# Output projection of the last layer: program order for 696 of its 768 products, squares, sums and turns at fixed products, splits moved out of the query blocks

## The chip, the cores and the metric

One core of one Trainium2 chip runs the whole step. The metric is the device time in microseconds (us) from start to end of one execution. The engines of the core are TensorE (PE in the profile, its weight loads PEld), VectorE (DVE), ScalarE (ACT), GpSimd (POOL) and SyncE (SP), which here issues the DMA transfers.

## The reference

A trunk of two layers is run once on a prompt (512 rows) and a sample (32 rows), 544 columns in all where the kernel works on the transposed rows. Layer 0 is RWKV-7 time mixing, layer 1 differential attention with 12 heads of width 128; both have cross-attention over 256 memory rows with 4 heads, and a gate. What the change touches is the end of layer 1 and the final norm:

```
def diff_layer(x, ...):
    h = rmsnorm(x, norm_w)
    q, k, v, qm, gate = split(h @ w_in)            # widths 1536, 1536, 1536, 512, 2048
    o = rmsnorm(diff_attention(q, k, v, lam), subln) * (1.0 - lam_init)
    y_mem = mem_attention(qm, mk, mv)
    out = concatenate([o, y_mem]) * silu(gate)     # 2048 columns
    return x + out @ w_out, k, v                   # w_out: 2048 x 1024

y_prompt = rmsnorm(xp, final_norm_w)
y_sample = rmsnorm(xs, final_norm_w)
```

## The kernel before

**Products.** Every product with weights is split into float16 halves: a weight block of 1024 rows and 128 columns becomes a high part (cast) and a low part (what the cast lost), and the activations likewise. A product with 128 weight rows is then three matmuls: high by high, high by low, low by high. The 544 columns are taken in two halves of 272, so a block is 2 x 8 x 3 = 48 matmuls; the text counts these matmuls as products. The accumulator of a half is one of three PSUM banks (`psg`).

**Weight stream.** `stream` runs all blocks of layer 1 one after the other: per head a value, a key and a query block, gate blocks (`GATES1`; head 11 has four) and, in heads 1, 3, 5 and 7, memory blocks; then the 16 blocks of the output projection. While PE works on block b, other engines prepare later ones, each step tied to a product of block b: two loads of 256 KB into one of four raw buffers (`LOADS1`, SP), the squares of a raw block for its scale (`square_total`, at products 14 and 27, ACT, written to `junkw`), a small matmul that sums them (`total_spread`, PE), four scalar operations that make a power of two of it (`scales`, at 32, DVE), the scaling of the raw block in two pieces (`scaled`, POOL), and in the block after that the split: two casts (ACT, at 7 and 11 in the output projection, `SPLITS2`), two low parts (POOL and DVE, at 13 and 17), written to `whs`. A raw buffer is free for the next load when its split is done.

**Heads.** `diff_layer` lists the work beside the stream as events, `at(position, function)`; a position is a product, counted from the start of the layer, and `begin(h)` is that of head h. Scores of a head in four tiles, maxima (`snm`, DVE), exponentials (ACT), the turned weights and the sums of values follow at fixed offsets, in the head after their own as a rule.

**Gated tiles.** `o1` holds 16 tiles of 128 rows and 544 columns, the concatenated output by its gate. Each is split too: `gated_square` (ACT) and `gated_scales` find a scale, `gated_split` casts the scaled tile (ACT, first half of `hl`), `gated_rest` takes the low half (DVE, second half of `hl`). For tiles 0 to 7 these are events of heads 8 to 11, the splits by the offsets `GSPLIT` from head 10; tiles 8 to 15 are split in the output projection.

**Output projection.** `make_out` (in `diff_layer`) does 8 column blocks k with tiles 0 to 7 (q = 0) and then 8 with tiles 8 to 15 (q = 1), 768 products. After each half `out_add` adds the accumulator to the residual `x1` (DVE), and with q = 1 calls `consume` (in `layer1`) for the final norm: `square_sums` squares the new `x1` (ACT, into `sqn`) and adds it to `sums` (DVE); after k = 3 all five row tiles are turned for their first 512 columns (four transposes each, PE, into `ps_f`, of which `psm` has two buffers) and multiplied by the norm's weight `fw` (DVE); later blocks are turned near the end, where `last` makes the root (`token_rms`) and writes the output. The block k = 6 of q = 1 has only its first half at its own place; its second half lies between the two halves of k = 7.

**Order.** While `ordered` is set, each engine keeps the order in which the program issues its instructions (`tie`). Where it isn't, the language's planner orders an engine's instructions by its own estimate of when each can start; `tied` keeps SP's order in all cases. `layer1` drives the projection's products with a counter `n` (768 at the end; the events of the heads still take its first 93). A list `left` holds functions by product: squares, scales and splits of tiles 8 to 15, and six pairs of copies of keys and values to the output (`kv_out`, SP). After product 384, the end of q = 0, `ordered` is cleared:

```
if n == KT * 6 * KT:
    self.ordered, self.tied = False, (self.se,)
```

Of the kernel before, what the change touches and what calls it, by code (L numbers as in the profile page):

```python
# [3 lines left out]

# [5 lines left out]
F32 = mybir.dt.float32  # L10
# [4 lines left out]
AF = mybir.ActivationFunctionType  # L15
ALU = mybir.AluOpType
AX = mybir.AxisListType

P = 128
D = 1024  # L20
KT = D // P
# [3 lines left out]
TH = T // 2  # L25
# [20 lines left out]
GSQUARE = ((8, 36), (8, 132), (9, 36), (9, 84), (10, 2), (10, 29), (10, 53), (10, 75))  # L46
GSCALE = ((9, 132), (10, 92))
KVOUT = 164
GSPLIT, GREST = (37, 66, 84, 115, 134, 180, 227, 252), 11
EXP = float(1 << 23)  # L50
ROOT = float(0x5F3759DF) + 14 * EXP
SAMPLE1 = ((310, "s"), (338, "m"), (362, "t"), (386, "w"), (406, "n"), (464, "r"))
# [87 lines left out]
class Trunk:  # L140
# [1711 lines left out]
    def layer1(self):  # L1852
        nc, a, o = self.nc, self.a, self.o
        w = a["df_in"][0]
        op = self.pool("o1", 1)
        self.o1 = [op.tile([P, T], F32, name=f"og{g}") for g in range(16)]
        with ExitStack() as ectx:
            tiles, late = {}, []
            with ExitStack() as c2:
                dq = self.pool("dq", 1)  # L1860
                p = self.pool("df", 1, ctx=c2)
                mctx = ExitStack()
                mp = self.pool("mem1a", 1, ctx=mctx, side="right")

                self.kz = [dq.tile([P, 2, T], F32R, name=f"kz{i}") for i in range(2)]
                for t in self.kz:
                    for m in range(2):
                        r = slice(64 - 64 * m, P - 64 * m)
                        nc.gpsimd.memset(t[r, m, :].bitcast(F32), 0.0)
                self.out = {x: dq.tile([P, n], F32, name=f"out{x}") for x, n in (("s", 16), ("m", 2), ("c", 2))}  # L1870
                self.out["t"] = dq.tile([P, 16], BF16, name="outt")
                self.out["r"] = dq.tile([P, 2, KT], F32, name="outr")
                self.out["f"] = dq.tile([P, 4, KT], F32, name="outf")
                main, n, kv_out = self.diff_layer(dq, p, mp, mctx, lambda: self.pool("wo1e", 1, ctx=ectx, side="right"), tiles,
                                                  lambda *x: self.out_add(late, *x))
            ctx = ectx.enter_context(ExitStack())
            po = self.pool("wo1", 1, ctx=ctx)
            p = self.pool("fin", 1, ctx=ctx, side="right")
            self.all_ones(p)
            fw = p.tile([P, D], F32, name="fw")  # L1880
            nc.scalar.dma_start(fw[:], a["final_norm_w"].unsqueeze(0).to_broadcast([P, D]))
            sums = p.tile([P, T], F32, name="sums")
            ya, yb = ([t[:, :512] for t in self.o1[i : i + 5]] for i in (0, 5))
            rows = [P] * 4 + [TS]

            held = {}

            def bank(i, q, g):
                held[i] = q.tile([P, 512], F32, tag=g, name="ps_f")

            def turned(i, ks):
                for k in ks:
                    c = min(i * P, T - P)
                    self.te.transpose(held[i][:, k % 4 * P : k % 4 * P + P], self.x1[:, k, c : c + P], self.ident[:])
                return slice(P - rows[i], P), held.pop(i) if ks[-1] % 4 == 3 else None

            def last(tiles):

                rs = self.token_rms(sums, p, tiles)
                for u, i in enumerate(tiles):  # L1900
                    if i == 3:
                        bank(3, self.psm, "m")
                    n, pf = turned(i, range(4, KT) if i == 3 else (KT - 1,))
                    r = rs[n, u : u + 1]
                    dst = o[0][0, i * P : i * P + P, :] if i < 4 else o[1][0]
                    self.ae.activation(ya[i][n], ya[i][n], AF.Copy, scale=r)
                    self.se.dma_start(dst[:, :512], ya[i][n])
                    self.ve.scalar_tensor_tensor(yb[i][n], pf[n, :], r, fw[n, 512:], ALU.mult, ALU.mult)
                    self.se.dma_start(dst[:, 512:], yb[i][n])

            def consume(k, x, v):
                self.square_sums((k, x, v), p, sums)
                if k == 3 and v.start:
                    for i in range(5):
                        bank(i, self.psm, "m")
                        n, pf = turned(i, range(4))
                        self.ve.tensor_tensor(ya[i][n], pf[n, :], fw[n, :512], ALU.mult)
                if k == KT - 2:
                    for i, q, g in (((2, self.psc, "c"), (4, self.psc, "c")) if v.start else ((0, self.psm, "m"), (1, self.psm, "m"))):
                        bank(i, q, g)  # L1920
                        turned(i, (4, 5, 6))
                if k == KT - 1:
                    last((2, 3, 4) if v.start else (0, 1))

            late.append(consume)
            order = (12, 13, 14, 15, 8, 9, 10, 11)
            left = [(24 + 12 * i, self.gated_square, g) for i, g in enumerate(order)]
            left += [(126, lambda g: self.gated_scales(g, 8), 8), (138, self.half_scale, 1)]
            left += [(150 + 24 * i, lambda g: self.gated_split(g, po, tiles), g) for i, g in enumerate(order)]
            left += [(160 + 24 * i, lambda g: self.gated_rest(g, tiles), g) for i, g in enumerate(order)]  # L1930
            left += [(KVOUT + 48 * i, lambda i: kv_out[i](), i) for i in range(len(kv_out))]
            left.sort(key=lambda x: x[0])
            for _ in main:
                n += 1
                while left and left[0][0] <= n:
                    _, fn, g = left.pop(0)
                    fn(g)
                if n == KT * 6 * KT:
                    self.ordered, self.tied = False, (self.se,)
        self.hctx.close()  # L1940

# [64 lines left out]
    def diff_layer(self, dq, p, mp, mctx, pool_early, tiles, consume):  # L2006
# [6 lines left out]
        rows = [slice(0, 64), slice(64, P)]  # L2013

        def at(pos, fn):
            ev.append((pos, len(ev), fn))

        def begin(h):
            return 6 * KT * sum(3 + len(GATES1.get(x, ())) + 2 * (x in MEM1) for x in range(h))
# [89 lines left out]
        def bank(m, name):  # L2109
            pool, tag = ((self.psx, "x"), (self.psc, "c"))[m]  # L2110
            return pool.tile([P, 512], F32, tag=tag, name=name)
# [25 lines left out]
        def joined(st, t):  # L2137
            mixed(*st["pt", t])
            if t == 3:
                s0 = st["G"]["s0"][:, 4 * st["j"] : 4 * st["j"] + 4]  # L2140
                self.ve.reciprocal(s0, s0)

        def turned(st, t):
            b0 = 2 * t * (t + 1)
            joined(st, t)
            self.ve.transpose(st["pk"][:, b0 : b0 + 4 * (t + 1)].rearrange("p b c -> p (b c)"), st.pop(("pt", t))[0])
# [37 lines left out]
        def squared(st):  # L2184
            j = st["j"]
            self.ve.tensor_reduce(st["G"]["ss"][:, 0, 4 * j : 4 * j + 4], st.pop("sq")[:], AX.X, ALU.add)
# [127 lines left out]
        for h, st in enumerate(sts):  # L2314
            f, hg, G = len(makes) * 6 * KT, h // 4, groups[h // 4]
# [18 lines left out]
            back, sums = (BACK2, SUMS2) if h >= DH - 2 else (BACK1, SUMS1)  # L2334
# [4 lines left out]
            if h in MEM1:  # L2339
                m = MEM1.index(h)  # L2340
# [3 lines left out]
            if h % 4 == 3:  # L2344
                for off, fn in (SAMPLE2 if last else SAMPLE1):
                    fn = {"s": sample_scores, "m": sample_mixed, "t": sample_turned, "w": sample_weighted, "n": sample_norm, "r": sample_rows}[fn]
# [3 lines left out]
                for j in range(4):  # L2350
# [6 lines left out]
                    else:  # L2357
                        x = b + 18 + STEP * j
# [4 lines left out]
            if h == 10:  # L2363
                we = []
                at(f + 34, lambda: (mctx.close(), we.append(pool_early())))
                for g, off in enumerate(GSPLIT):
                    at(f + off, lambda g=g: self.gated_split(g, we[0], tiles))
                    at(f + off + GREST, lambda g=g: self.gated_rest(g, tiles))
        for g, (h, off) in enumerate(GSQUARE):
            at(begin(h) + off, lambda g=g: self.gated_square(g))  # L2370
        for g, (h, off) in zip((0, 4), GSCALE):
            at(begin(h) + off, lambda g=g: self.gated_scales(g, 4))
        at(begin(11) + 40, lambda: self.half_scale(0))
# [2 lines left out]
        first = len(makes) * 6 * KT  # L2376
# [30 lines left out]
        i = 0  # L2407
# [94 lines left out]
```

## Time and profile before

| What | us |
|---|---|
| Median of 3 runs (lowest to highest) | 1365.05 (1363.4 to 1370.18) |
| Profiled execution, its whole time | 1367.86 |
| its span, from the first to the last instruction | 1366.0 |
| PE busy | 1300.2 |
| DVE busy | 945.2 |
| ACT busy | 887.7 |
| POOL busy | 679.6 |

The profile is that of one execution, so its times are compared with its own span, and results with the runs. "Idle before, releaser" behind an instruction tells how long its engine had stood and which instruction's end let it go on. In the weight stream ps_g is the accumulator, ps_s the scores, whs a split weight block, h16s the raw blocks and their scales, hl a split gated tile, og a tile of `o1` (its room serves the output later), qp the query.

### The profile page before, as it was taken

Reading aid. Unit: us, or ns where it says so; the run is one execution under the profiler, and the core shown is the slowest. Engines: PE = TensorE matmul, PEld = TensorE weight load, DVE = VectorE, ACT = ScalarE, POOL = GpSimd, SP = SyncE. Lnnn points to the kernel's source line nnn. Section 1 sums busy time; section 2 is a strip of 40 time slices with the busy share of each in tenths; the row PEclk is TensorE's granted clock in tenths of the full one; section 3 lists DMA queues with packets and bytes.
Section 4 is the critical chain, followed back from the end, with each engine's and each line's share of the span. In section 5 each row is a group of like instructions: output and inputs, shape, how many; then the busy total and the mean of one; then the engine's idle time right before and its main releaser. Section 6 shows DMA issues by size and latency. Waiting matters only on the chain. (4 is left out here: it accounts for less than half of the span.)

```text
span 1366.0 us, 32365 instructions
## 1 busy us (share of the span) xinstructions
PE 1300.2 (95%) x11776; PEld 1170.6 (86%) x11776; DVE 945.2 (69%) x2477; ACT 887.7 (65%) x2412; POOL 679.6 (50%) x1145
## 2 busy tenths in 40 slices
PE   6998999999999999999999999999999999999987
PEld 6898889999999999888899997788878887778865
DVE  7766667877788778756683463666697667877745
ACT  7665777677777777665653356767766777775642
POOL 2216765568556755660120028665565655553641
PEclk9999999999999999999999999999999999999998
DMA  7542223322332232233366445767777868683731
GB/s 242 174 125 69 60 70 87 79 75 68 86 78 72 73 87 74 67 96 88 109 208 190 129 143 138 167 150 171 163 172 155 187 144 196 152 174 84 257 96 66
DMA packets 418298, 171.55 MB, mean 126 GB/s; under 512 B 195209, under 2 KB 402578, under 8 KB 418138
## 3 DMA queue, kind: packets, MB, share of 16 engines
q1 hardware_dynamic: 417994, 168.96, 47.9%
q8 instruction: 93, 1.52, 0.5%
q14 instruction: 67, 0.55, 0.1%
q10 hardware_dynamic: 144, 0.52, 0.1%
HBM read 130.84 MB, written 41.92 MB: 126 GB/s over the span
## 5 line engine op out<-in xcount | busy, mean ns | idle before, releaser
L137 PEld LDWEIGHTS <-whs 128*128 128x128 f16 x3456 | 330.2, 99 | 76.8 <-POOL whs L137 8.0
L137 PE MATMUL ps_g<-h,whs 128*128 128x272 f16 x2688 | 337.2, 282 | 3.5 <-POOL whs L137 3.5
L137 PE MATMUL ps_g<-hh,wlo 128*128 128x272 f32 x912 | 277.1, 304 | 1.2 <-DVE wlo L137 1.2
L137 PE MATMUL ps_g<-hh,whi 128*128 128x272 f32 x912 | 274.3, 301 | 0.9 <-ACT hh L137 0.9
L137 PE MATMUL ps_g<-hl,whi 128*128 128x272 f32 x912 | 270.9, 297 | 0.6 <-POOL hl L600 0.5
L889 POOL TENSOR_TENSOR tm<-u,m 102x84 f32<-102x84 f32 (+23 forms) x372 | 159.3, 428 | 165.3 <-DMA m<-sc 134.4
L137 POOL TENSOR_TENSOR whs<-h16s,whs 128x512 f16<-128x512 f32 x128 | 149.1, 1182 | 63.8 <-ACT whs L137 62.2
L137 PEld LDWEIGHTS ps_g<-hh,whi 128*128 128x128 f32 x912 | 174.1, 191 | 4.4 <-ACT hh L137 1.3
L137 PEld LDWEIGHTS ps_g<-hh,wlo 128*128 128x128 f32 x912 | 173.6, 190 | 4.7 <-DVE wlo L137 2.0
L137 PEld LDWEIGHTS ps_g<-hl,whi 128*128 128x128 f32 x912 | 173.5, 190 | 2.4 <-POOL hl L600 0.7
L891 POOL TENSOR_TENSOR u<-u,tm 102x84 f32<-102x84 f32 (+23 forms) x372 | 159.5, 429 | 29.1
L137 DVE TENSOR_TENSOR wlo<-raw,whi 128x512 fp32r<-128x512 f32 x178 | 129.3, 737 | 47.4 <-ACT whi L137 46.5
L137 ACT CAST whi<-raw 128x512 fp32r<-128x512 f32 x178 | 107.1, 616 | 35.8 <-issue 19.3
L137 POOL TENSOR_SCALAR h16s<-h16s 128x512 f32<-128x512 f32 x112 | 78.8, 715 | 96.7 <-DVE h16s L137 89.1
L137 ACT CAST whs<-h16s 128x512 f16<-128x512 f32 x144 | 84.2, 617 | 31.0 <-POOL h16s L137 25.5
L137 PE MATMUL ps_g<-hl,whs 128*128 128x272 f16 x768 | 93.8, 279 | 3.3 <-POOL whs L137 2.2
L137 ACT ACTIVATE junkw<-h16s 128x512 bf16<-128x512 f32 x138 | 86.6, 627 | 9.4 <-DMA h16s<-in_w_out_dram 9.0
L137 DVE SCALAR_TENSOR_TENSOR SB<-ps_c,dl,sd 64x64 f32<-64x64 f32 x168 | 47.4, 282 | 43.0 <-PE ps_c L137 38.6
L137 PE MATMUL ps_g<-lo,whi 128*128 128x272 f32 x256 | 73.9, 289 | 0.7 <-DVE lo L137 0.7
L137 PE MATMUL ps_g<-hi,whi 128*128 128x272 f32 x256 | 73.7, 288 | 0.0
L137 PE MATMUL ps_g<-hi,wlo 128*128 128x272 f32 x256 | 73.6, 288 | 0.0
L137 ACT COPY sv<-ps_c 64x64 f32<-64x64 f32 x192 | 39.2, 204 | 39.2 <-PE ps_c L137 37.4
(413 smaller groups left out, 2926.6 us busy)
## 6 DMA issues: line engine op xcount, KB each, us to landing
raw<-in_rw_in_dram SPq DMA_DIRECT2D x114, 256.0 KB
h16s<-in_df_in_dram SPq DMA_DIRECT2D x112, 256.0 KB
raw<-in_w_out_dram SPq DMA_DIRECT2D x32, 256.0 KB
h16s<-in_w_out_dram SPq DMA_DIRECT2D x32, 256.0 KB
ptr<-pk SPq DMA_DIRECT2D x44, 160.0 KB
aT<-ptr SPq DMA_DIRECT2D x11, 640.0 KB
scr<-sg SPq DMA_DIRECT2D x96, 68.0 KB
out_dram<-scr SPq DMA_DIRECT2D x6, 1024.0 KB
```

Of the source, the lines that this page charges most:

```text
L137: return lambda *a, **k: self.trunk.tie(self, issue(*a, **k))
L889: nc.gpsimd.tensor_tensor(tm[:, :n, :wd], u3[:, :n, kx : kx + 1].to_broadcast(sh), m3[:, kx : kx + 1, kx + 1 :].to_broadcast(sh), ALU.mult)
L891: nc.gpsimd.tensor_tensor(u3[:, :n, kx + 1 :], u3[:, :n, kx + 1 :], tm[:, :n, :wd], ALU.add)
```

## The change

Three edits go together.

- The splits of tiles 0 to 7 get places by head and product, one for the cast and one for the low half, instead of offsets from head 10 with a fixed distance of 11. The casts move from products 37, 66, 84, 115, 134, 180, 227 and 252 of head 10 (which has 144, head 11 follows) to 36 and 66 of head 10 and 33, 66, 165, 222, 254 and 290 of head 11; the low halves follow by 7 to 24 products.
- `ordered` is cleared at product 696 (`ORDERED`) instead of 384. From there 72 products are left: the two halves of k = 7 and the second of k = 6.
- In `consume` the square is issued one product later and its sum eight products later, through the list `left`, which can now take new entries while it runs; the first turns of row tile i are issued at 6 + 14 i products behind k = 3, and the product with `fw` 7 behind them, where before all five stood together. The squares and sums of the last three halves stay at once.

```diff
-from itertools import chain
+from itertools import chain, count
-GSPLIT, GREST = (37, 66, 84, 115, 134, 180, 227, 252), 11
+GSPLIT = ((10, 36, 57), (10, 66, 89), (11, 33, 57), (11, 66, 89), (11, 165, 172), (11, 222, 230), (11, 254, 262), (11, 290, 298))
+ORDERED = (2 * KT - 2) * 6 * KT + 3 * KT
...
-            held = {}
+            held, left, ticket = {}, [], count()
+
+            def after(off, fn, g):
+                left.append((n + off, next(ticket), fn, g))
+
+            def squared(x):
+                k, t, v = x
+                sq = sums[:, v]
+                if k:
+                    held["sq"] = p.tile([P, TH], F32, tag="sqn", name="sqn", bufs=2)
+                    sq = held["sq"][:]
+                self.ae.activation(sq, t, AF.Square)
+
+            def summed(v):
+                self.ve.tensor_tensor(sums[:, v], sums[:, v], held["sq"][:], ALU.add)
+
+            def first(i):
+                bank(i, self.psm, "m")
+                held["p", i] = turned(i, range(4))
+
+            def weighed(i):
+                rows, pf = held["p", i]
+                self.ve.tensor_tensor(ya[i][rows], pf[rows, :], fw[rows, :512], ALU.mult)
...
             def consume(k, x, v):
-                self.square_sums((k, x, v), p, sums)
                 if k == 3 and v.start:
                     for i in range(5):
-                        bank(i, self.psm, "m")
-                        n, pf = turned(i, range(4))
-                        self.ve.tensor_tensor(ya[i][n], pf[n, :], fw[n, :512], ALU.mult)
+                        after(6 + 14 * i, first, i)
+                        after(13 + 14 * i, weighed, i)
+                if k < KT - 2 or k == KT - 2 and not v.start:
+                    after(1, squared, (k, x, v))
+                    if k:
+                        after(8, summed, v)
+                else:
+                    squared((k, x, v))
+                    summed(v)
...
-            left.sort(key=lambda x: x[0])
             for _ in main:
                 n += 1
+                left.sort()
                 while left and left[0][0] <= n:
-                    _, fn, g = left.pop(0)
+                    _, _, fn, g = left.pop(0)
                     fn(g)
-                if n == KT * 6 * KT:
+                if n == ORDERED:
                     self.ordered, self.tied = False, (self.se,)
...
-                for g, off in enumerate(GSPLIT):
-                    at(f + off, lambda g=g: self.gated_split(g, we[0], tiles))
-                    at(f + off + GREST, lambda g=g: self.gated_rest(g, tiles))
...
+        for g, (h, x, y) in enumerate(GSPLIT):
+            at(begin(h) + x, lambda g=g: self.gated_split(g, we[0], tiles))
+            at(begin(h) + y, lambda g=g: self.gated_rest(g, tiles))
```

The left-out lines fill `left` with the same functions at the same products as before.

More of the change, by code (lines that the diff above doesn't have):

```diff
@@ L1925, in layer1 @@
             late.append(consume)
[L1926 to L1931, printed above, removed]
-            left.sort(key=lambda x: x[0])
+            n0, n = n, 0
+            for i, g in enumerate((12, 13, 14, 15, 8, 9, 10, 11)):
+                after(24 + 12 * i, self.gated_square, g)
+                after(150 + 24 * i, lambda g: self.gated_split(g, po, tiles), g)
+                after(160 + 24 * i, lambda g: self.gated_rest(g, tiles), g)
+            after(126, lambda g: self.gated_scales(g, 8), 8)
+            after(138, self.half_scale, 1)
+            for i in range(len(kv_out)):
+                after(KVOUT + 48 * i, lambda i: kv_out[i](), i)
+            n = n0
             for _ in main:
                 n += 1
+                left.sort()
                 while left and left[0][0] <= n:
-                    _, fn, g = left.pop(0)
+                    _, _, fn, g = left.pop(0)
                     fn(g)
-                if n == KT * 6 * KT:
+                if n == ORDERED:
                     self.ordered, self.tied = False, (self.se,)
```

## The prediction

> **What bounds the kernel now.** I read the page first, then the busy time by stretch of the span, then who TensorE (PE) waited for, then the timeline of the two places where it did.
>
> ```profile
> span 1366.0 us, 32365 instructions
> PE 1300.2 (95%) x11776; PEld 1170.6 (86%) x11776; DVE 945.2 (69%) x2477; ACT 887.7 (65%) x2412; POOL 679.6 (50%) x1145
> ```
>
> PE is busy 95% of the span, so only its 65.8 idle us, or work taken from it, can be won. The change takes no instruction away. The question is which of its idle time lies in the code that is touched: the weight stream of heads 10 and 11 (about 1170 to 1245 us) and the output projection behind it. Rows of the stretches (stretch, length, then busy us and count of PE, PEld, DVE, ACT, POOL, then PE clock, DMA share, GB/s):
>
> ```profile
> 1194.00:1197.00 3.00, 0.79 (x7) 0.42 (x5) 2.71 (x7) 0.81 (x5) 1.48 (x2) 1.00 0.65 102
> 1197.00:1200.00 3.00, 2.88 (x18) 2.26 (x19) 1.93 (x10) 2.42 (x8) 1.36 (x2) 0.75 0.91 156
> 1200.00:1203.00 3.00, 3.00 (x21) 2.17 (x20) 2.89 (x12) 2.10 (x7) 0.49 (x1) 0.68 0.16 48
> 1203.00:1207.00 4.00, 4.00 (x35) 3.35 (x33) 2.87 (x10) 3.88 (x12) 3.15 (x4) 1.00 0.50 75
> ...
> 1270.00:1298.10 28.10, 28.10 (x260) 23.76 (x258) 20.08 (x46) 17.95 (x41) 19.06 (x16) 1.00 0.85 275
> 1298.10:1331.20 33.10, 26.35 (x230) 20.74 (x228) 16.22 (x39) 14.19 (x34) 15.20 (x14) 1.00 0.30 95
> 1331.20:1339.70 8.50, 8.50 (x80) 7.19 (x79) 5.61 (x17) 2.35 (x5) 3.33 (x3) 1.00 0.01 2
> ```
>
> Two holes stand out. **Hole A:** PE idles around 1195, and then runs at a granted clock of 0.75 and 0.68 until 1203. **Hole B:** in 1270 to 1298.1 PE starts one instruction per 28.10 / 260 = 0.108 us without a gap; the 230 instructions of 1298.1 to 1331.2 would take 24.9 us at that pace and take 33.1, so 8.2 us are lost. Where in the program are we there? PE's groups of 1298.1 to 1331.3, and then those from 1339.76 to the end:
>
> ```profile
> L137 PE MATMUL ps_g<-hl,whs 128*128 128x272 f16 x194 | 24.6, 279 | 3.3 <-POOL whs L137 2.2 <-ACT whs L137 1.0
> L137 PE MATMUL ps_f<-ident,x 128*128 128x128 f32 x20 | 3.2, 283 | 3.4 <-DVE og L137 2.0 <-DVE h16s L137 1.4
> ```
> ```profile
> L137 PE MATMUL ps_g<-hl,whs 128*128 128x272 f16 x109 | 13.8, 279 | 0.0
> ```
>
> The projection has 768 products, so with 109 left (one of them at the edge) 1339.76 is product 660; 8.50 us earlier, three halves of 24 products at full pace, is 588; with the 192 between (194 with the edges) hole B runs from product 396 to 588. Program order is given up at product 384. A half is 2.83 us, a block 5.66.
>
> **Hole B, its cause.** Who PE waited for in 1296 to 1332, then the timeline (start, us, engine, op, count, idle before and releaser):
>
> ```profile
> PE ps_g L137 <- POOL whs L137: 2.2, 3, 0.8
> PE ps_f L137 <- DVE og L137: 2.0, 2, 1.2
> PE ps_f L137 <- DVE h16s L137: 1.4, 1, 1.4
> PE ps_g L137 <- ACT whs L137: 1.0, 1, 1.0
> ```
> ```profile
> 1295.27 0.93 SPq L137 DMA_DIRECT2D h16s<-in_w_out_dram  x2
> ...
> 1296.92 2.04 POOL L137 TENSOR_TENSOR h16s<-h16s,outf 128x512 f32<-128x512 f32 x2 [1.68 <-DVE outf L137]
> ...
> 1300.58 0.63 ACT L137 ACTIVATE junkw<-h16s 128x512 bf16<-128x512 f32 x1 [3.34 <-DMA h16s<-in_w_out_dram]
> ...
> 1301.96 1.12 ACT L137 CAST whs<-h16s 128x512 f16<-128x512 f32 x2
> ...
> 1302.64 1.15 POOL L137 TENSOR_TENSOR whs<-h16s,whs 128x512 f16<-128x512 f32 x1 [3.69 <-ACT whs L137]
> ...
> 1303.82 15.15 SPq L137 DMA_DIRECT2D h16s<-in_w_out_dram  x6
> ...
> 1303.85 1.33 PE L137 MATMUL ps_g<-hl,whs 128*128 128x272 f16 x10 [0.82 <-POOL whs L137]
> ```
>
> POOL had scaled the block's weights by 1299 (1296.92 + 2.04). ACT casts them only at 1301.96, because a square of a later block's weights (junkw) stands ahead of the casts and waits 3.34 us for its transfer, issued at 1295.27. PE then stands for the low halves that follow the casts. In the written order a block has its casts at products 7 and 11 and that square at 14. So the planner's order, not the transfer, makes this wait; the late cast also keeps the raw buffer and puts off the next load to 1303.82. By the first list that is 2.2 + 1.0 = 3.2 us. The other 3.4 us are at the turns of x1 for the final norm: 20 transposes in one lump at product 576, through two buffers that DVE empties (DVE og).
>
> **Hole A, its cause.**
>
> ```profile
> 1186.52 0.73 ACT L137 ACTIVATE hl<-og,outs 128x544 f16<-128x544 f32 x1
> ...
> 1189.48 1.03 DVE L137 SCALAR_TENSOR_TENSOR qp<-ps_g,h16s,qp 64x272 fp32r<-64x272 f32 x2 [2.10 <-ACT qp L137]
> ...
> 1190.54 0.79 DVE L137 SCALAR_TENSOR_TENSOR hl<-og,outs,hl 128x544 f16<-128x544 f32 x1
> ...
> 1194.91 1.15 DVE L137 SCALAR_TENSOR_TENSOR hl<-og,outs,hl 128x544 f16<-128x544 f32 x1
> ...
> 1196.29 0.49 DVE L137 TENSOR_REDUCE snm<-ps_s 128x1 f32<-128x128 f32 x2
> ...
> 1196.61 0.37 ACT L137 ACTIVATE pt<-ps_s,snm 128x128 f32<-128x128 f32 x1 [2.19 <-DVE snm L137]
> ...
> 1197.12 0.39 PE L137 MATMUL ps_s<-kh,qp 128*128 128x256 f32 x1 [2.33 <-ACT pt L137]
> ```
>
> Read upward: PE's next scores need the bank that ACT's exponential empties, that needs the maximum (snm), and DVE comes to it late: two low halves of gated tiles (hl) lie before it, and before those DVE waited 2.10 us for a query evacuation on ACT, behind an hl cast.
>
> **The change part by part.** *Splits.* The eight casts (ACT, 0.73 us) and low halves (DVE, 0.79 to 1.15 us) stay eight each and issue no DMA. Counted from head 10, the casts move from products 37, 66, 84, 115, 134, 180, 227, 252 to 36, 66, 177, 210, 309, 366, 398, 434. Between product 96 and the scores of 156 none is left. DVE reaches snm earlier by 0.79 + 1.15 = 1.94 us, and by up to 0.73 us more as the evacuation it waited for comes sooner: 2.67 against the 2.33 of the stall. I take the stall as gone but for 0.3 us. The slow clock goes with it: (1 - 0.75) x 2.88 + (1 - 0.68) x 3.00 = 1.7 us. Gain 2.3 + 1.7 - 0.3 = **3.7 us**. Late there next is the cast of the block's weights, for which nothing waits yet. Four splits now lie in head 11's gate blocks, where PE waits once:
>
> ```profile
> PE ps_aT L137 <- DVE pt L137: 1.1, 1, 1.1
> ```
>
> ```profile
> 1218.61 0.60 ACT L137 ACTIVATE ps_o<-ot 128x512 f32<-128x512 f32 x1 [2.08 <-DVE ot L137]
> ...
> 1233.26 0.69 DVE L137 TENSOR_TENSOR ot<-ps_o,os 128x512 f32<-128x512 f32 x1 [1.61 <-PE ps_o L137]
> ```
>
> ACT and DVE wait up to 2.08 and 1.61 us at a time there, which covers one split at a time; without that cover each costs up to its 0.73 + 1.15 us. Bounds of this part: from a gain of 4.0 + 1.1 (this wait goes too, since the query block before it has lost its split) to a loss of 1.0 (hole A's stall moves, and one split is not covered). I take 3.7, nearest to the rows of the chain.
>
> [...]
>
> *Program order to product 696.* ACT's squares of later weights no longer come ahead of the casts, so the 3.2 us go. Added are waits in fixed places: ACT's square of x at one product behind a half waits for DVE's evacuation, and behind it on ACT stand the next casts; DVE's sum at 8 products waits for that square, and behind it stands the chain of four scalar operations that releases POOL. The loop that sets the weights' pace, from the rows of 1296.7 to 1345 (mean ns before the bar):
>
> ```profile
> L137 DVE TENSOR_TENSOR whs<-h16s,whs 128x512 f16<-128x512 f32 x7 | 8.0, 1145 | 17.3 <-ACT whs L137 17.3
> L137 DVE SCALAR_TENSOR_TENSOR x<-ps_g,h16s,x 128x272 f32<-128x272 f32 x14 | 6.9, 495 | 3.3 <-PE ps_g L137 3.3
> L137 DVE TENSOR_TENSOR sums<-sums,sqn 128x272 f32<-128x272 f32 x10 | 5.1, 512 | 1.5 <-ACT sqn L137 1.5
> L137 ACT CAST whs<-h16s 128x512 f16<-128x512 f32 x14 | 8.0, 612 | 5.5 <-PE ps_g L137 3.7 <-POOL h16s L137 1.8
> L137 ACT ACTIVATE sqn<-x 128x272 f32<-128x272 f32 x11 | 4.7, 428 | 13.2 <-DVE h16s L137 10.0 <-DVE x L137 3.2
> ```
>
> POOL scales 2.1, last cast 0.61, low half 1.15, x 0.50, square 0.43, sum 0.51, the chain's four operations about 0.8 (an estimate: none of them reaches 0.25 in the timeline), handoffs some 0.3: 6.6 us a block, where PE takes 5.66. The lag grows 0.9 us a block over blocks 9 to 11, from 2.1 (POOL starts at 1296.92, its place is product 368, about 1294.8). PE stands only above some 4.2: from POOL's place to the block's use are 64 products, 7.5 us, less POOL's 2.1 and 1.15 (the low half). So 2.1 + 3 x 0.9 = 4.8 passes that by 0.6 at block 11; the transposes of blocks 12 and 13 then give PE more to do. The last block comes 24 products sooner, since the one before has only half its products there: I take 1.0 us for both.
>
> *Turns at own places.* Twenty transposes, now 14 products (1.6 us) apart, with each product with fw 7 behind. The products with fw on DVE (min/median/max ns):
>
> ```profile
> L137 DVE TENSOR_TENSOR og<-ps_f,fw x5: 678/681/696, 1326.7 to 1331.6; 128x512 f32<-128x512 f32 x4, 32x512 f32<-32x512 f32 x1
> ```
>
> DVE needs 0.68 us for one, two buffers give it 3 us: the 3.4 us go, the transposes' 20 x 0.11 us are in the 24.9 already.
>
> Sum of hole B: 8.2 less 1.0 for those two and 0.7 for waits on the evacuation at the turns: **6.5 us**. Bounds: 8.2 and nothing. The tail behind product 696 keeps its freedom. Together 3.7 + 6.5 = 10.2: the profiled execution of 1367.86 (span 1366.0, 1.9 around it) would be 1357.7, and the median of 1365.05 becomes 1354.9.
>
> **The rivals.** *The stall of A only moves* (0.14): head 11's chain of maximum, exponential and join takes the splits' 1.9 us each time; against it stand ACT's and DVE's waits for PE there. Hole B alone: 1365.05 - 6.5 = 1358.5. *The order starves PE in B* (0.18): the loop is 7.5 us and more, or loads issued at the old times are late in the new order too, as the 3.34 us wait for DMA hints; then only the lump's 3.4 and 3.7 of A come: 1358.0, and with a loop still longer 1361.4. *The clock stays* (0.06), by the slow rows having another cause: 2.0 + 6.5, 1356.6. *Slower* (0.10): the loop passes 8 us, because ACT's square, waiting for DVE behind POOL's chain, holds up the casts instead of running beside POOL. From a wait of 2.3 us a block on, PE would pay as in hole A, 2.3 + 1.7, over six blocks 24 us in place of 8.2: 1365.05 + 15.8 - 3.7 = 1377. It needs 1.4 us more a block than I add up.
>
> **How the numbers follow.** The forecast has 0.52, and 1354.9. Range 1351.5 to 1361.5: below it both holes close and the wait in head 11 too (5.1 + 8.2 gives 1351.8); above it lie the slower case and some of the second rival. About 0.5% (6.8 us) is what can be told from no change, so faster means below 1358.2: the forecast, the clock, half of the first rival, a third of the second, 0.71; slower 0.08 (of the 0.10, some ends within 0.5%); the same 0.21.
>
> **What would show it.** PE's wait for ACT pt at the second scores of head 11 gone, and clock 1.00 there; between products 396 and 588 some 25 to 27 us in place of 33.1; no square of weights ahead of casts on ACT; transposes in five groups. Wrong would be: PE waits for POOL whs in every block of the second half, or a new wait of 2 us in head 11.

## The result, and the profile after

| | Median, us | Lowest to highest | Ratio to before (95%) |
|---|---|---|---|
| before | 1365.12 | 1362.62 to 1370.18 | |
| changed | 1357.09 | 1356.08 to 1359.37 | 0.9936 (0.9914 to 0.9958) |

The change is worth 8.0 us by the medians (5.7 to 11.7 by the interval of the ratio), where 10.2 were forecast. A second series, e12 below, gave a ratio of 0.9946 (0.9926 to 0.9965). One execution of e6 below ran at a granted clock of 0.56 and took 2117.3 us; its ratio leaves that one out. The page of the changed kernel:

```profile
span 1353.3 us, 32365 instructions
PE 1295.5 (96%) x11776; PEld 1169.4 (86%) x11776; DVE 948.2 (70%) x2477; ACT 888.7 (66%) x2412; POOL 678.0 (50%) x1145
```

The two profiled spans differ by 12.7 us, more than the medians. The surplus arose before any changed instruction. PE's wait for the second set of turns of the outputs of heads 4 to 7 (ps_oT, at product 10 of head 10, 1.7 to 1.8 us in every run here) lies ahead of all the splits, and the change leaves it alone. The matmul that sums the squares of tiles 8 to 15 (ps_gs, product 126 of the projection) lies behind all the splits of tiles 0 to 7 and ahead of hole B. These two points cut the span (start, us, op, idle before). Before:

```profile
1164.65 0.66 PE L137 MATMUL ps_oT<-ident,ot 128*128 128x128 f32 x4 [1.69 <-DVE og L137]
...
1266.22 0.17 PE L137 MATMUL ps_gs<-outt,h16s 128*128 128x8 bf16 x1 [0.59 <-ACT junkw L137]
```

Changed:

```profile
1160.29 0.66 PE L138 MATMUL ps_oT<-ident,ot 128*128 128x128 f32 x4 [1.70 <-DVE og L138]
...
1260.56 0.17 PE L138 MATMUL ps_gs<-outt,h16s 128*128 128x8 bf16 x1 [0.60 <-ACT junkw L138]
```

The changed kernel came to the first point 4.4 us sooner, in code that the change doesn't touch. The clock can account for it: up to there it stood at 0.50 for seven stretches of 3.41 us before (one from 1133.66 on) and for four after; at half of a stretch each, an estimate, three fewer are 5.1 us. From there **stretch A**, to ps_gs, took 101.6 before and 100.3 after; **stretch B**, from ps_gs to the end of the span, 99.8 and 92.7. So stretch A won 1.3 us in this pair and the projection 7.0: 8.3 together, near the 8.0 of the medians. All runs below are read by these stretches, since they leave out what happens earlier.

**Hole B is closed.** PE's small sums for the scales are 24 products apart; those of products 396 and 660, before and then after:

```profile
1298.07 0.19 PE L137 MATMUL ps_g<-h16s 128*128 128x1 bf16 x2
...
1339.71 0.19 PE L137 MATMUL ps_g<-h16s 128*128 128x1 bf16 x2
```
```profile
1292.41 0.19 PE L138 MATMUL ps_g<-h16s 128*128 128x1 bf16 x2
...
1325.73 0.19 PE L138 MATMUL ps_g<-h16s 128*128 128x1 bf16 x2
```

41.6 us became 33.3 for the same 264 products and 20 transposes. Of the waits in hole B that the prediction listed, for casts and low halves (whs) and at the lump, none is left. PE's waits from 1262 to the end of the changed kernel are these:

```profile
PE ps_f L138 <- DVE x L138: 1.0, 3, 0.6
PE ps_n L138 <- DVE sums L138: 0.5, 1, 0.5
PE ps_g L138 <- POOL whs L138: 0.4, 1, 0.4
```

All of them lie behind product 660, where the changed kernel lost 1.3 us again (27.6 to the end for 26.3): the 0.4 for whs is new, and of the 1.0 for x 0.5 is.

**Hole A has moved.** The wait for ACT pt at head 11's second scores is gone, and PE is busy all of 1190 to 1210 at full clock, but two other waits stand in the timeline:

```profile
1215.69 0.33 PE L138 MATMUL ps_aT<-ident,pt 128*128 128x128 f32 x1 [2.89 <-DVE pt L138]
...
1237.36 0.63 PE L138 MATMUL ps_aT<-ident,pt 128*128 128x128 f32 x4 [0.87 <-DVE os L138]
```

Before, they were 1.05 and none. Ahead of the first, on ACT and on DVE:

```profile
1212.08 0.74 ACT L138 ACTIVATE hl<-og,outs 128x544 f16<-128x544 f32 x1
1212.72 0.48 ACT L138 ACTIVATE og<-ps_g,h16s 128x272 f32<-128x272 f32 x1
```
```profile
1213.23 0.44 DVE L138 SCALAR_TENSOR_TENSOR og<-og,ps_g 128x272 f32<-128x272 f32 x1 [1.66 <-ACT og L138]
1213.59 0.78 DVE L138 SCALAR_TENSOR_TENSOR hl<-og,outs,hl 128x544 f16<-128x544 f32 x1
...
1215.28 0.35 DVE L138 SCALAR_TENSOR_TENSOR pt<-ps_s,srs,pt 128x128 f32<-128x128 f32 x1
```

A moved cast holds up the gate's evacuation (og) on ACT, for which DVE waits 1.66 us, and its low half then holds up the join (pt) on DVE. That is tile 4's split, at products 165 and 172 of head 11; the join is at 180.

### The profile page after: what moved, and what is told of

It reads as the page before. It is cut to its first block, busy times and chain, and to the rows that moved or that the text cites. A ratio compares the mean times of both kernels' runs of the same rounds, so it can differ in the third digit from the quotient of the medians.

```text
span 1353.3 us, 32365 instructions
## 1 busy us (share of the span) xinstructions
PE 1295.5 (96%) x11776; PEld 1169.4 (86%) x11776; DVE 948.2 (70%) x2477; ACT 888.7 (66%) x2412; POOL 678.0 (50%) x1145
## 5 line engine op out<-in xcount | busy, mean ns | idle before, releaser
L138 PE MATMUL ps_g<-h,whs 128*128 128x272 f16 x2688 | 331.1, 279 | 3.6 <-POOL whs L138 3.6
```

The costliest lines, as they stand in the source:

```text
L138: return lambda *a, **k: self.trunk.tie(self, issue(*a, **k))
```

## The experiments

Theory: the projection's part works as forecast; the splits' gain at the second scores is mostly given back at the joins. Rivals: the splits bring it all, or nothing, or help the projection. The columns A and B are the stretches defined above, in us; "clock" says where in A the granted clock fell, in rows of 10 us.

| Run | Median | Ratio (95%) | A | clock | B |
|---|---|---|---|---|---|
| before | 1365.12 | | 101.6 | 1190 to 1210 | 99.8 |
| changed | 1357.09 | 0.9936 (0.9914 to 0.9958) | 100.3 | full | 92.7 |
| e1_splits | 1365.81 | 1.0003 (0.9985 to 1.0020) | 103.0 | 1210 to 1230 | 100.5 |
| e2_projection | 1359.34 | 0.9957 (0.9943 to 0.9971) | 101.6 | full | 92.8 |
| e3_order | 1362.08 | 0.9974 (0.9957 to 0.9991) | 101.6 | 1190 to 1200 | 96.4 |
| e4_places | 1365.76 | 0.9999 (0.9981 to 1.0018) | 101.7 | full | 97.8 |
| e5_behind | 1353.95 | 0.9909 (0.9896 to 0.9923) | 98.2 | full | 92.8 |
| e6_two | 1365.96 | 0.9997 (0.9982 to 1.0012) | 102.0 | 1220 to 1230 | 99.0 |
| e7_sums | 1355.45 | 0.9909 (0.9892 to 0.9927) | 98.2 | full | 91.9 |
| e8_all | 1362.33 | 0.9977 (0.9963 to 0.9992) | 101.6 | 1210 to 1220 | 95.8 |
| e9_turn | 1353.65 | 0.9921 (0.9896 to 0.9945) | 99.2 | 1160 to 1180 | 92.8 |
| e10_turn_sums | 1355.81 | 0.9923 (0.9901 to 0.9945) | 97.8 | full | 91.9 |
| e11_splits_behind | 1360.43 | 0.9963 (0.9948 to 0.9978) | 98.3 | full | 98.3 |
| e12_changed_again | 1358.93 | 0.9946 (0.9926 to 0.9965) | 101.8 | 1210 to 1220 | 92.8 |

The ratios are to the kernel before in the same series: e1 to e4, e5 to e8 and e9 to e12 ran on one chip each, with medians of 1365.11, 1365.72 and 1366.67 before. A and B come from one profiled execution of each kernel, which need not be a typical one: the changed kernel's is the fastest of its six, e1's the slowest of its twelve, e9's the slowest of its six, e12's the fastest of its ten.

**e1_splits**, the first part alone (with the loop that places the splits, as in the change):

```diff
-GSPLIT, GREST = (37, 66, 84, 115, 134, 180, 227, 252), 11
+GSPLIT = ((10, 36, 57), (10, 66, 89), (11, 33, 57), (11, 66, 89), (11, 165, 172), (11, 222, 230), (11, 254, 262), (11, 290, 298))
```

> Only the splits at their new places; the projection as before. Theory 1 (the stall of head 11's second scores goes, and about two thirds of that comes back as longer waits for the joined weights, ps_aT, in head 11's gate blocks): no wait of PE for ACT pt at the second scores, ps_aT waits of 2.9 and 0.9 us, and 1.3 us less than before, 1363.8. Rival (the splits bring the whole 3.7 us of the prediction): 1361.4. Rival (they bring nothing): 1365.1.

No gain that can be told (2.0 us less to 2.7 more), where the theory had 1.3. The waits are as expected:

```profile
1220.66 0.47 PE L137 MATMUL ps_aT<-ident,pt 128*128 128x128 f32 x1 [2.90 <-DVE pt L137]
...
1245.06 0.63 PE L137 MATMUL ps_aT<-ident,pt 128*128 128x128 f32 x4 [0.88 <-DVE os L137]
```

But in this execution the clock fell at the first of them, as this row of 10 us shows (0.68 in the clock's column, 58 matmuls where the changed kernel has 98):

```profile
1220.00:1230.00 10.00, 9.34 (x58) 7.25 (x59) 4.27 (x19) 5.97 (x20) 4.67 (x6) 0.68 0.94 244
```

It is 0.32 x 9.34 = 3.0 us, and stretch A is 103.0 where the changed kernel has 100.3. What the other eleven executions paid, no trace here shows.

**e2_projection**, the second and third part alone, with the old `GSPLIT` and its loop.

> Only the projection's part (order to product 696, squares, sums and turns at own places); the splits as before. Theory 1: hole B closes, some 6.6 us less, 1358.5, with the 2.3 us wait at head 11's second scores as before. Rival (part of the gain comes from the splits freeing DVE and ACT in time): under 5 us less.

5.9 us by the ratio (4.0 to 7.8), stretch B 92.8 as in the whole change: the splits give nothing to the projection. It also holds the answer on the clock before. Its PE rows in stretch A:

```profile
1198.14 0.38 PE L138 MATMUL ps_s<-kh,qp 128*128 128x256 f32 x1 [2.33 <-ACT pt L138]
...
1220.68 0.45 PE L138 MATMUL ps_sc<-ckT,qs 64*32 64x128 f32 x16 [0.45 <-ACT pt L138]
...
1223.76 0.33 PE L138 MATMUL ps_aT<-ident,pt 128*128 128x128 f32 x1 [1.77 <-DVE pt L138]
```

The same stall of 2.33 us, but here full clock behind it; and PE then waits 0.45 + 1.77 instead of 1.05. Stretch A is 101.6 either way. The same pair comes again in e3 (slow clock, then 1.07 at the join) and e4 (full clock, then 0.45 + 1.76), with 101.6 and 101.7. So the slow clock before cost nothing, because the join further on was late anyway.

**e3_order**, only the point at which order is given up:

```diff
-                if n == KT * 6 * KT:
+                if n == (2 * KT - 2) * 6 * KT + 3 * KT:
```

> Only the product at which order is given up, 696 for 384; the five turns still in one lump, squares and sums at once. Theory 1: the waits for casts and low halves go (3.2 us), those at the lump stay or grow, since PE can put no products between: 2 to 3.5 us less, 1361.5 to 1363. Rival (the planner's order is the whole cause): 6 us and more. Rival (written order without the places starves PE): no gain or slower.

3.5 us (1.2 to 5.9), as the theory had it. All waits for whs are gone; the lump remains:

```profile
PE ps_f L137 <- DVE og L137: 1.8, 2, 1.6
PE ps_f L137 <- DVE x L137: 1.0, 3, 0.6
```

Behind the lump the clock fell to 0.83 from 1320 to 1330, another 1.7 us, in this execution.

**e4_places**, the new places of squares, sums and turns, order given up at 384:

```diff
-ORDERED = (2 * KT - 2) * 6 * KT + 3 * KT
+ORDERED = KT * 6 * KT
```

> Only the places of squares, sums and turns; order still given up at product 384, splits as before. Theory 1: the lump's 3.4 us go and the wait behind the square that stands for its transfer stays: 3 us less, 1362. Rival (the planner reorders whatever it is given): no difference, 1365.

No gain that can be told in time (2.6 us either way), so the theory's 3 us didn't come. But the rival's reason isn't what the trace shows. The five turns keep places of their own, some 2.1 us apart, PE's waits at the lump (2.0 + 1.4) are gone, and B is 97.8 for 99.8, although the clock fell in it (0.83 from 1310 to 1320, 1.7 us). Why the twelve executions show nothing of this is open. The waits for whs stay, 1.5 + 1.1 us for the 3.2 before. ACT again stands for a transfer ahead of the casts, at two blocks by some 3 us, as it did before (3.34, and 3.18 at 1308.39):

```profile
1298.64 0.63 ACT L138 ACTIVATE junkw<-h16s 128x512 bf16<-128x512 f32 x1 [2.87 <-DMA h16s<-in_w_out_dram]
...
1306.61 0.63 ACT L138 ACTIVATE junkw<-h16s 128x512 bf16<-128x512 f32 x1 [3.32 <-DMA h16s<-in_w_out_dram]
1307.14 0.19 ACT L138 ACTIVATION_READ_ACCUMULATOR junkw<-h16s 128x1 bf16 x1
1307.37 0.63 ACT L138 ACTIVATE junkw<-h16s 128x512 bf16<-128x512 f32 x1
1307.90 0.19 ACT L138 ACTIVATION_READ_ACCUMULATOR junkw<-h16s 128x1 bf16 x1
1308.00 1.12 ACT L138 CAST whs<-h16s 128x512 f16<-128x512 f32 x2
```

With the written order kept, the places bring what e2 has over e3: 92.8 against 96.4 in B, of which 1.7 is e3's clock. By their times e2 and e3 can't be told apart (0.9943 to 0.9971, 0.9957 to 0.9991).

**e5_behind**, the change with two splits behind the joins they held up:

```diff
-... (11, 165, 172), ... (11, 290, 298))
+... (11, 193, 203), ... (11, 306, 318))
```

> The changed kernel with two splits moved on: tile 4's from products 165 and 172 of head 11 to 193 and 203, tile 7's from 290 and 298 to 306 and 318, each behind the join that PE waited for. Theory 1 (a cast of 0.74 us on ACT and a low half of 0.8 to 1.0 us on DVE stand ahead of those joins): the ps_aT waits fall from 2.9 and 0.9 to about 1.5 and 0, some 2.2 us less than the changed kernel, 1355. Rival (PE is only earlier, the join is bound by what lies before it): the waits and the time stay, 1357.

Faster than before, 0.9909 (0.9896 to 0.9923), and by its ratio some 4 and 5 us better than the changed kernel's two series (0.9936 and 0.9946; the interval of the first overlaps). The one wait that is left at the joins, with full clock behind it:

```profile
1215.92 0.33 PE L138 MATMUL ps_aT<-ident,pt 128*128 128x128 f32 x1 [1.54 <-DVE pt L138]
```

Stretch A falls by 2.1 us against the changed kernel's own profile, by 3.6 against e12's, in which the clock fell. So these two splits made the longer waits at the joins.

**e6_two**, the kernel before with tiles 3 and 4 split at 309/316 and 366/374 from head 10, the others as they were:

```diff
-GSPLIT, GREST = (37, 66, 84, 115, 134, 180, 227, 252), 11
+GSPLIT = ((37, 48), (66, 77), (84, 95), (309, 316), (366, 374), (180, 191), (227, 238), (252, 263))
```

> The kernel before with only the two splits of head 10's query block moved (tile 3's to 309 and 316, tile 4's to 366 and 374, counted from head 10). Theory 1: these two alone made the 2.3 us wait at head 11's second scores; it goes or falls under 0.5 us, and the wait at ps_aT grows: 0.5 to 2 us less, 1363.5. Rival (the stall comes from the backlog of all five splits in head 10): a wait of over 1 us stays.

The stall at the second scores is gone altogether, so these two splits made it. The time isn't: PE meets the late join instead, and the clock fell there too (0.83).

```profile
1219.04 0.45 PE L137 MATMUL ps_sc<-ckT,qs 64*32 64x128 f32 x16 [0.45 <-ACT pt L137]
1223.45 0.33 PE L137 MATMUL ps_aT<-ident,pt 128*128 128x128 f32 x1 [3.09 <-DVE pt L137]
```

**e7_sums**, e5 with the sums later:

```diff
-                        after(8, summed, v)
+                        after(12, summed, v)
```

> The kernel of the run before last with the sums 12 products behind their half in place of 8, so behind the chain of scalar operations that releases POOL. Theory 1 (the loop of 6.0 us a block over PE's 5.66 makes the one 0.4 us wait for POOL whs): POOL's starts come 5.7 apart, the wait goes, 0.2 to 0.5 us less than that kernel. Rival: no difference that can be told.

In time no difference from e5 that can be told; in the profile stretch B is 0.9 shorter and the wait for whs is gone. POOL's starts on the raw weights (h16s) in the changed kernel, then in e7:

```profile
1296.09 2.04 POOL L138 TENSOR_TENSOR h16s<-h16s,outf 128x512 f32<-128x512 f32 x2 [1.68 <-DVE outf L138]
...
1302.21 2.04 POOL L138 TENSOR_TENSOR h16s<-h16s,outf 128x512 f32<-128x512 f32 x2 [2.62 <-DVE outf L138]
...
1308.24 2.04 POOL L138 TENSOR_TENSOR h16s<-h16s,outf 128x512 f32<-128x512 f32 x2 [2.68 <-DVE outf L138]
```
```profile
1301.96 2.16 POOL L138 TENSOR_TENSOR h16s<-h16s,outf 128x512 f32<-128x512 f32 x2 [1.68 <-DVE outf L138]
...
1307.63 2.17 POOL L138 TENSOR_TENSOR h16s<-h16s,outf 128x512 f32<-128x512 f32 x2 [1.68 <-DVE outf L138]
```

6.1 and 6.0 us apart where PE needs 5.66 a block; with the sums out of the loop 5.67.

**e8_all**, order kept to the last product:

```diff
-ORDERED = (2 * KT - 2) * 6 * KT + 3 * KT
+ORDERED = 2 * KT * 6 * KT
```

> The changed kernel with order kept to the last product. Theory 1 (the last 72 products have turns and norm sums that wait for DVE, and the planner puts products between): PE waits for sums and x in the open, 2 to 4 us more than the changed kernel, 1360. Rival: no difference, 1357.

0.9977, against 0.9936 and 0.9946 of the changed kernel: some 4 to 6 us slower. Against the changed kernel's first profile, stretch B is some 3 us longer, and A 1.3, where the clock fell in this execution. PE stands for two evacuations and two sums of the norm, where in the changed kernel the planner put products between:

```profile
PE ps_n L138 <- DVE sums L138: 3.3, 2, 1.7
PE ps_f L138 <- DVE x L138: 2.1, 2, 1.6
```

**e9_turn** and **e10_turn_sums** are e5 and e7 with the first turn of head 11's joined weights 14 products later:

```diff
-                    at(f + y + 12, lambda st=st, t=t: turned_here(st, t))
+                    at(f + y + (26 if t == 0 else 12), lambda st=st, t=t: turned_here(st, t))
```

> The run with the two splits behind the joins, and head 11's first turn of joined weights (ps_aT, one transpose) 14 products later, at 206 of the head. Theory 1 (PE still waits 1.5 us there because DVE's chain up to the join is longer than PE's work): PE does those products meanwhile, the wait goes but for what then waits for the bank of the next scores, 0.5 us at most: 1 us less than that run, 1353. Rival (the wait only moves to the next scores): the same time as that run.

> The run before with the sums 12 products behind their half in place of 8: no wait for POOL whs in the second half of the projection, 0.4 us less, 1352.5. Rival: no difference that can be told.

The wait of 1.5 us goes, and one of 1.08 comes at the sample's turn (ps_saT, for DVE pt). Neither is told from e5 by its time (0.9921 and 0.9923, intervals 0.9896 to 0.9945), so nothing is claimed for them.

**e11_splits_behind**, e1 with e5's two places:

> The splits alone, projection as before, with the places that lie behind the joins. Theory 1 (the splits' gain at the second scores was given back in front of the joins and, in some executions, by a lower granted clock behind the 2.9 us wait): a wait of 1.5 us at ps_aT, full clock behind it, 3 us less than before, 1362. Rival (the splits have nothing to give): 1365.5.

5.1 us (3.0 to 7.1), where e1 had nothing, over the expected 3. PE waits 1.56 us at ps_aT with full clock behind it, and the wait at the second scores is gone. Stretch A, 98.3, is 3.3 below before; B came out at 98.3 too, with the projection unchanged (99.0 to 100.5 in before, e1 and e6), so some 1.5 us of this one profile are not the splits'.

**e12_changed_again**, the changed kernel beside the last three:

> The changed kernel itself on the same chip as the other three, for their differences: 1357. Theory 1 on the clock: behind the 2.9 us wait at ps_aT the granted clock is 1.00 in some executions and lower in others, so this may be one of either kind.

The same waits as in its first profile (2.90 and 0.87), but here the clock fell at the first, to 0.83 over 10 us, 1.7 us; stretch A is 101.8 instead of 100.3.

## Why the prediction was right, and where it wasn't

The time lies within the range, and the sign and most of the size came as forecast. It did so by hole B: the 6.5 us forecast there give 1358.5 alone, and what the splits added can't be told from nothing by the runs (e1: 2.0 us less to 2.7 more; the whole change against e2: 0.9936 and 0.9957, with overlapping intervals). By its steps:

- **Hole B's cause held.** "The planner's order, not the transfer, makes this wait": e3 removes all waits for whs by order alone, and e4, with order given up, has them again. The rival of starving loads is out: with the order kept, ACT never waits for a transfer in B.
- **Its sum held**, in part by errors that offset each other: 6.5 forecast, 7.0 in the stretch. The terms written down for the loop add up to 6.4 us a block, not 6.6, and it measured 6.0 to 6.1. Of the "1.0 us for both" of lag and last block, 0.4 came (the wait for whs at 1330.97); of the 0.7 for evacuations at the turns, 0.56 came, at a turn behind product 660 (1331.93). The 3.4 us of the lump were priced as coming from the places alone; e4 loses those waits, but no time that can be told.
- **Hole A's cause held**: e6 moves only the two splits named, and the stall goes.
- **Hole A's size was the failing step.** "I take the stall as gone but for 0.3 us. The slow clock goes with it", "late there next is the cast of the block's weights, for which nothing waits yet". The stall went, but the next late thing was the join in head 11 (ps_aT), already waited for before. Of the 3.7 us, the clock's 1.7 couldn't be had while that join was late (e2 has full clock and the same 101.6), and tile 4's split in front of the join, with tile 7's before a later one, took back most of the rest: 1.3 in the profile with full clock, nothing or less when the clock falls (e12, e1). The prediction's own sign of being wrong, "a new wait of 2 us in head 11", nearly came: 1.05 became 2.89, and 0.87 is new. With these two splits behind the joins the splits do bring 5.1 us (3.0 to 7.1, e11), so a gain of about the forecast size was there for the splits, at other places. The first rival, "the stall of A only moves", given 0.14, describes what happened to A: it gave 1358.5 for the whole.
- **The cover was misjudged.** ACT's and DVE's waits of 2.08 and 1.61 us in head 11 were taken as room for a split. They end when something arrives; a split placed behind that arrival gets none of it. At 165 and 172 the instructions stood behind such a wait and ahead of the join, as the rows at 1212.08 and 1213.59 show.

The forecast lets the slow clock go with the stall, the rival in which the clock stays gives it another cause. The runs agree with neither reading as it stands: stalls of 2.33 us had a slow clock behind them in two profiles of four (before, e3; not e2, e4), stalls of 2.9 in three of four (e1, e8, e12; not the first profile after), and the one of 3.09 in e6 had it too. The last section shows what parts them.

## What to carry to other kernels

When a stall is priced, walk on to the next thing the stalled engine will wait for: if that is late already, only the smaller of the two gains is there, and a slow clock between them may cost nothing (stretch A is 101.6 us before, with it, and in e2, without). Idle time of a helper engine is room only for what is placed before the event that ends it. Where a planner may reorder, a place keeps the turns apart but not the casts ahead of a square that waits for its transfer (e4); keep the written order where a queue would block on a transfer (e3), and leave it free where the last steps wait on each other (e8).

## What the runs showed of the hardware

The granted clock fell at waits of PE well under 3 us, and not every time: 1.58 us at e3's lump, 1.70 in e9 at ps_oT (0.84 from 1160 to 1170, where the other thirteen profiles have none behind the same wait), 2.33 and 2.9 as above. In rows of 0.1 us such a fall is a stretch of 3.41 us at 0.50 (before, from 1133.66 and from 1198.51), or two on end (6.83, before from 171.10, e1 from 1219.59). That is the 0.83 in a row of 10 us, and up to 1.7 us lost, in e1 3.0. Within an execution the stretches begin on one grid of 3.413 us: 1133.66 and 1198.51 before are 64.85 us or 19 of them apart, 1194.89 and 1321.19 in e3 126.30 us or 37.

With the grid of each trace (in before, 1195.10 to 1198.51 is the stretch ahead of the fall at the second scores), the busy share of PE in the stretches that the wait touches parts the executions that pay from those that don't:

| Profile | Wait of PE, us | PE's busy share in the emptiest stretch of the grid | Clock in the next |
|---|---|---|---|
| before | 2.33 | 0.41 | 0.50 |
| e3 | 2.33 | 0.32 | 0.50 |
| e2 | 2.33 | 0.52 | 1.00 |
| e4 | 2.33 | 0.64 | 1.00 |
| e12 | 2.90 | 0.22 | 0.50 |
| e1 | 2.90 | 0.47 | 0.50 |
| changed | 2.89 | 0.51 | 1.00 |
| e6 | 3.09 | 0.32 | 0.50 |

A wait that falls within one stretch empties it, and one that lies across a border is shared between two: of the 2.33 us before, 2.02 lie in the stretch from 1195.10, while the changed kernel's 2.89 lie 1.68 and 1.21 us to either side of 1214.48. In these rows a busy share of 0.47 and less had a slow stretch behind it, and 0.51 and more had none. Between them lie, worked out from the rows of PE, the stretches ahead of e3's fall at the lump (0.49) and of e9's at ps_oT (about 0.50, an estimate from its clocks of 0.84 and 0.99 over the two rows of 10 us from 1160), so the rows set no sharp border. From 1000 to 1345 us of before and of the changed kernel, two stretches have a share under 0.47 (0.40 and 0.41, both before) and a slow one behind them, and none of the others, from 0.51 on, has. So whether a wait of 2.33 to 2.90 us was paid for hung, in these profiles, on where it lay on the grid. This is read from the traces; no run set out to shift a wait on the grid, and earlier in the span falls came behind fuller stretches too, which this doesn't explain: 0.83, 0.98 and 0.57 before (falls at 171.10, 311.05 and 877.66), 0.93 and 0.98 in the changed kernel (173.41 and 309.95).
